# A two-stream decoder step: the sample's decode steps issued at another pace, the prompt's values multiplied over 512 columns

## The chip, the cores and the metric

One core of a Trainium2 chip runs one program. The metric is the device time of one execution in microseconds (us), read as the median of several runs of the same kernel.

## The reference

The program is one inference step of a two-layer decoder for two streams of tokens with the same weights (1024 channels, 16 heads of 64, 4096 hidden units). The **prompt** has 512 tokens, the **sample** 8 sequences of 4 new tokens, each with 2048 past keys and values in a paged cache. Layer 0 is a convolution module and an MLP. Then one key/value projection is made from the residual stream, and layer 1 is stick-breaking attention (query projection, attention, output projection) and another MLP. Cut to the part around the change:

```
k_flat, v_flat = split(x @ w_kv, 2)                 # x: after layer 0
q  = (x*(1+scale)+shift) @ attn_wq
z  = einsum('bqhd,bkhd->bhqk', q, k) * 64**-0.5 + bias[head]
log_rem = where(k_pos < q_pos, log_sigmoid(-z), 0)  # stick breaking, instead of a softmax
after   = exclusive suffix sum of log_rem over the keys
w  = where(k_pos < q_pos, exp(log_sigmoid(z) + after), 0)
o  = einsum('bhqk,bkhd->bqhd', w, v) @ attn_wo
x  = layer_norm(alpha*x + (1+gate)*o)               # post-norm; then the MLP in the same form
```

Everything is float32. The new keys and values of both streams are outputs too. scale, shift and gate come from small products of a condition vector with large matrices ("ada" below).

## The kernel before, in words

**Prompt.** Activations lie channel by channel: eight tiles of 128 channels by 512 tokens. To keep float32 accuracy each operand is split in two float32r parts, hi (a cast) and lo (the rest), and each product is three matmuls, hi*hi, hi*lo and lo*hi (`mm3`, L326 to L331; tile name `pd`). Weights come as 1 MB tiles `stage` (three buffers, loaded from ScalarE's DMA queue) and are split by `wsplit` (L312): ScalarE casts `whi` (L316), VectorE subtracts `wlo` (L319), two buffers each. `make_h` (L441) writes the split input of the next projection, `xhi` on ScalarE (L454), a helper `h` (L456), `xlo` on VectorE (L460); it takes the eight buffers of the projection before, so a block is written when its last reader is done.

The stages follow each other: convolution, LN (layer normalisation), `pw2`, LN, MLP 0 (eight blocks `fb`), LN, keys (K, eight tiles `pd`), values (V, L1346 to L1365), queries (Q), attention over eight head pairs (L1385 to L1441), output projection, LN, MLP 1 with a tail. The values are the one projection computed with tokens in the partitions: x is the stationary side and the weights are the moving side. They are made in four groups c of 256 columns; in each, for two pairs of token blocks, one PSUM bank `pv` takes two blocks of 128 tokens x 256 columns, with the eight blocks k of channels innermost. A bank is copied (`vN`, L1361) and written to two places in DRAM: `vd`, from which attention reads a head pair's values, and the output.

**Attention of a head pair** (a `pr`): TensorE makes the scores `pz` in three units of query blocks, ScalarE takes two sigmoids of them (L1414, L1416), VectorE a running product from the right (`TENSOR_TENSOR_SCAN`, L1423) and a product (L1424), TensorE transposes the weights (`awt`), ScalarE copies them (`aw`), TensorE multiplies with the values (`oP`), ScalarE and VectorE split the result (L1439, L1440).

**Sample.** Its dense layers stream large weights past 32 tokens. Its attention is a run of decode steps, four key steps and four value steps for each of the eight sequences. A key step `dec_keys` gathers two 1 MB tiles `kraw` from the cache (L1043, on GpSimd's queue; the same ring of four buffers that all the sample's weights use), transposes them on VectorE in eight pieces (`kt`, L1065) and makes scores `zt` with 64 matmuls (L1071). A value step `dec_values` gathers two tiles `vt` and makes 16 matmuls `av` (L1122). After four key steps `dec_weights` turns a sequence's scores into weights. Before the fourth sequence (counted from 0) 16 ada steps come (`ada_b_(1)`, `ada_a(1, 1)`: each a 1 MB load on SyncE's queue, and matmuls L246) whose results the prompt needs after attention. The transposes are ordered behind the last `xlo` of the last `make_h` (`latest_sub`), the decode matmuls behind the last prompt matmul noted in `latest`, which before is set by `mm3` alone, so not in the values or in attention.

**Order.** Both streams are Python generators, merged by two issue clocks (L1495 to L1509): each `yield` adds a cost to its stream's clock, and the stream whose clock is behind goes on. `DEC_COST` is the cost of a decode step, `SMP_COST` 2.9 that of a dense or ada step of the sample, `DN_COST` 5.2 that of a tile of a prompt projection, `AT_COST` that of a head pair, an MLP block costs 41.6. The costs so decide beside which prompt work a decode step is issued. Within that order a scheduler places each instruction when its planned inputs are ready; each engine then runs its own queue in order.

```
        i = 0 if (alive[0] and (not alive[1] or clock[0] <= clock[1])) else 1
        ...
            cost = next(gens[i])
        ...
                clock[i] += cost
```

Of the kernel before, what the change touches and what calls it, by code (L numbers as in the profile page):

```python
# [17 lines left out]
P = 128  # L18
D = 1024
KT = 8  # L20
# [7 lines left out]
CW = 31  # L28
NPG = 16
NPOOL = 160  # L30
DEC_COST = 10.0
CLK0 = -20.0
EARLY = 0
SMP_COST = 2.9
# [16 lines left out]
LN_COST = 16.0  # L51
DN_COST = 5.2
ML_COST = 2.6
AT_COST = 12.0
ALPHA = 4.0 ** 0.25
EPS = 1e-5
QSC = 0.125
# [54 lines left out]
def yoco_step_kernel(  # L112
# [9 lines left out]
    nc = tc.nc  # L122
    mm = nc.tensor.matmul
# [3 lines left out]
    dma = nc.sync.dma_start  # L127
# [14 lines left out]
    def pm(name="pm"):  # L142
        return ps.tile([P, 512], F32, tag="pm", bufs=3, name=name)

    def aux(name="aux"):
        return ps.tile([P, 512], F32, tag="aux", bufs=4, name=name)

    def lnp(name):
        return ps.tile([P, 512], F32, tag="ln", bufs=1, name=name)
# [7 lines left out]
    def tmp(name="tmp"):  # L157
        return pp.tile([P, 512], F32, tag="tmp", bufs=4, name=name)
# [145 lines left out]
    def wstage(src, k, queue=nc.scalar, after=None):  # L304
        st = wp.tile([P, 2048], F32, tag="stage", bufs=STB, name="stage")
        ins = queue.dma_start(st.rearrange("p (k c) -> p k c", k=k), src.rearrange("(k p) c -> p k c", p=P))
        if after:
            order(ins, after[-1])
            after.append(ins)
        return st.rearrange("p (k c) -> p k c", k=k)  # L310

    def wsplit(st, c0, cw, wp=wp, after=None, chain=None):  # L312
        k = st.shape[1]
        hi = wp.tile([P, k, cw], F32R, tag="whi", bufs=2, name="whi")
        lo = wp.tile([P, k, cw], F32R, tag="wlo", bufs=2, name="wlo")
        ins = nc.scalar.copy(hi, st[:, :, c0 : c0 + cw])  # L316
        if after:
            order(ins, after)
        ins = vec.tensor_tensor(lo, st[:, :, c0 : c0 + cw], hi.bitcast(F32), op=ALU.subtract)  # L319
        if chain is not None:  # L320
            in_turn(chain, ins)
        return hi, lo

    latest = []
# [8 lines left out]
    def order(ins, after):  # L333
        tc.add_manual_dep(ins.ins, after.ins.name,
                          mybir.DependencyInfo(mybir.DependencyClass.NoSync, mybir.DependencyReason.DATA), reason="issue order")
        return ins
# [76 lines left out]
    def in_turn(chain, ins):  # L413
        if chain:
            order(ins, chain[-1])
        chain.append(ins)
# [366 lines left out]
    for c in range(4):  # L783
        st = []
# [7 lines left out]
        accs = []  # L792
# [7 lines left out]
        if c == 0:  # L800
            p1c = ExitStack()
            plc = pool(p1c, "p1c", "right")
            accs = [pm("pw1") for _ in range(3)] + [aux("pw1")]
            ws = [None] * 4
# [36 lines left out]
            for k in range(KT):  # L841
                t = tmp("ax0")
# [11 lines left out]
        for i in range(2):  # L854
            kt = 2 * c + i
            if c:
                ws = [wsplit(st[o], i * P, P) for o in range(2)]
                accs = [pm("pw1") for _ in range(2)]
# [37 lines left out]
    for g in range(4):  # L896
        r = slice(32 * g, 32 * g + 32)
# [5 lines left out]
    def sample():  # L903
# [143 lines left out]
        def dec_keys(s, f, st):  # L1047
            if f == 0:
                qb = sq.tile([P, 2, 16, 8, NQ], F32, tag="qb", bufs=1, name="qb")
                for u in range(2):  # L1050
                    vec.tensor_tensor(
                        qb[:, u],
                        qr.rearrange("p (b t) -> p b t", t=32)[:, u * 16 : u * 16 + 16, s * 4 : s * 4 + 4].unsqueeze(2).to_broadcast([P, 16, 8, NQ]),
                        mqb.rearrange("p (b x q) -> p b x q", x=8, q=NQ), op=ALU.mult)
                st["qb"], st["zt"] = qb, [aux("zt") for _ in range(2)]
            qb, zt = st["qb"], st["zt"]
            raw = [ring("kraw") for _ in range(2)]
            for x in range(2):
                gather(raw[x], cache_k, krow[:, s, f, x : x + 1])
            for u in range(2):  # L1060
                for hh in range(2):
                    kt = sq.tile([P, 4, 256], F32, tag="kt", bufs=KTB, name="kt")
                    c0 = u * 512 + hh * 256
                    for x in range(2):
                        ins = vec.transpose(kt[:, 2 * x : 2 * x + 2, :], raw[x].rearrange("p (e c) -> p e c", e=2)[:, :, c0 : c0 + 256])  # L1065
                        if latest_sub and DBH:
                            order(ins, latest_sub[0])
                    for dd in range(2):
                        for g in range(4):
                            bl = g * 2 + dd  # L1070
                            behind(mm(  # L1071
                                zt[u][32 * g : 32 * g + 32, f * P : f * P + P],
                                qb[:, u, hh * 8 + bl].rearrange("p x q -> p (x q)"),
                                kt[:, :, bl * 32 : bl * 32 + 32],
                                start=(hh == 0 and dd == 0), stop=(hh == 1 and dd == 1), tile_position=(0, 32 * g)))
# [36 lines left out]
        def dec_values(s, a, st):  # L1112
            if a == 0:
                st["av"] = aux("av")
            av, wT = st["av"], st["wT"]
            for i in range(2):
                vt = ring("vt")
                gather(vt, cache_v, vrow[:, s, a, i : i + 1])
                for e in range(2):
                    for u in range(2):  # L1120
                        g = 2 * u + e
                        behind(mm(av[32 * g : 32 * g + 32, :], wT[u][:, i, e, a, :],  # L1122
                                  vt[:, e * D + u * 512 : e * D + u * 512 + 512],
                                  start=(a == 0 and i == 0), stop=(a == 3 and i == 1), tile_position=(0, 32 * g)))
            if a < 3:
                return
            am = sq.tile([P, 512], F32, tag="z_s", bufs=2, name="am")
            vec.tensor_tensor(am, av, bmask, op=ALU.mult)
            ot = aux("ot")
            for c in range(4):  # L1130
                mm(ot[:, c * 8 : c * 8 + 8], am[:, c * P : c * P + P], selq, start=True, stop=True)
            o = oT.rearrange("p (u c) t -> p u c t", u=2)[:, :, :, s * 4 : s * 4 + 4]
            vec.tensor_tensor(o, o, ot[:, 0:32].rearrange("p (c u q) -> p u c q", c=4, u=2), op=ALU.add)

        sts = [{} for _ in range(NS + 1)]
        for s in range(NS + 1):
# [5 lines left out]
            for f in range(4):  # L1142
                if s < NS:
                    dec_keys(s, f, sts[s])
                    yield DEC_COST
                if s > 0:
                    dec_values(s - 1, f, sts[s - 1])
                    yield DEC_COST
            if s < NS:
# [100 lines left out]
    def prompt():  # L1250
# [79 lines left out]
        nv_out = new_v_prompt[0].rearrange("(i p) h d -> p i (h d)", p=P)  # L1330
        vd_v = vd.rearrange("(i p) c -> p i c", p=P)
# [11 lines left out]
            dma(nk_out[:, ts.start // P : ts.stop // P, kt * P : kt * P + P], kn.rearrange("p (i c) -> p i c", i=n))  # L1343

        yield from p_dense_out(w_kv[:, 0:D], xhi, xlo, fink, first=H_0B)
        for c in range(4):  # L1346
            st = wstage(w_kv[:, D + c * 256 : D + c * 256 + 256], KT)
            ws = [wsplit(st[:, 4 * r : 4 * r + 4, :], 0, 256) for r in range(2)]
            for i2 in range(2):
                a = pm("pv")  # L1350
                for ii in range(2):
                    i = i2 * 2 + ii
                    o = a[:, ii * 256 : ii * 256 + 256]
                    for k in range(KT):
                        whi, wlo = [w[:, k % 4, :] for w in ws[k // 4]]
                        xh, xl = xhi[k][:, i * P : i * P + P], xlo[k][:, i * P : i * P + P]
                        mm(o, xh, whi, start=(k == 0), stop=False)
                        mm(o, xl, whi, start=False, stop=False)
                        mm(o, xh, wlo, start=False, stop=(k == KT - 1))
                t = tmp("vN")  # L1360
                nc.scalar.copy(t, a)  # L1361
                tv = t.rearrange("p (i c) -> p i c", i=2)
                dma(vd_v[:, 2 * i2 : 2 * i2 + 2, c * 256 : c * 256 + 256], tv)
                dma(nv_out[:, 2 * i2 : 2 * i2 + 2, c * 256 : c * 256 + 256], tv)
                yield DN_COST  # L1365
        yield from need("abA10")
        a10, b10 = mods["abA10"]
# [17 lines left out]
        for pr in range(KT):  # L1385
            qT, kT, vN = qts[pr], tmp("kTr"), tmp("vNr")
            dma(kT, kd[pr])
            vN = vN.rearrange("p (i c) -> p i c", i=4)
            dma(vN, vd_v[:, :, pr * P : pr * P + P])
            oP = lnp("oP")  # L1390
            for unit in units:
# [13 lines left out]
                for i, c0 in unit:  # L1405
                    for r, z in zip(halves, zs):
                        order(mm(z[:, c0 : c0 + (i + 1) * P], qT[r, i * P : i * P + P], kT[r, 0 : (i + 1) * P], start=False,
                                 stop=False, skip_group_check=True), head)
# [10 lines left out]
                for s, fx in sfs:  # L1419
# [8 lines left out]
                    w = att.tile([P, T], F32, tag="aw", bufs=2, name="aw")  # L1428
# [11 lines left out]
            vec.tensor_tensor(olo[pr], oP, ohi[pr].bitcast(F32), op=ALU.subtract)  # L1440
            yield AT_COST  # L1441
        p3.close()
# [55 lines left out]
    while any(alive):  # L1498
        i = 0 if (alive[0] and (not alive[1] or clock[0] <= clock[1])) else 1
# [42 lines left out]
```

## Time and profile before

| | |
|---|---|
| time, median of 3 runs | 1649.34 us (1648.95 to 1651.52) |
| the profiled execution | 1650.69 us; span from first to last instruction 1648.9 us |
| TensorE (PE) busy | 1553.3 us, 94% of the span |
| VectorE (DVE) busy | 954.8 us, 58% |
| ScalarE (ACT) busy | 569.4 us, 35% |
| mean granted TensorE clock | 0.979 of 2.4 GHz |
| DMA | 409.24 MB, mean 248 GB/s |

A busy time is the sum of an engine's instructions in a stretch, without counting overlaps twice. The granted clock is 1.0 at 2.4 GHz and 0.5 at 1.2 GHz; a value between is a mean over the stretch. In a row of a timeline, what stands in brackets is the time that the engine stood idle just before, and what ended it. Matmul ends are modelled, so the pace of matmuls is read from their starts.

### The profile page before, as it was taken

What the parts mean: (1) busy time and instruction counts of PE and PEld (TensorE: products, weight loads), DVE (VectorE), ACT (ScalarE), POOL (GpSimd) and SP (SyncE); (2) the same over time, 40 slices, a digit from 0 to 9 for tenths busy, and PEclk for the clock granted to TensorE, in tenths of its full rate; (3) what the DMA queues carried; (4) which work ended last, traced back from release to release, by engine and by line L of the source; (5) the groups of instructions that cost most, each with busy time, mean ns of one, the idle gap of its engine ahead of it and who ended that gap; (6) DMA issues with size and microseconds to landing.
All of it is one profiled execution on the core that took longest, in us unless ns stands there. A gap on an engine that the chain in (4) does not pass through costs nothing.

```text
span 1648.9 us, 25461 instructions
## 1 busy us (share of the span) xinstructions
PE 1553.3 (94%) x10489; PEld 1088.2 (66%) x10489; DVE 954.8 (58%) x1818; ACT 569.4 (35%) x907; POOL 181.2 (11%) x201
## 2 busy tenths in 40 slices
PE   6999989989999999999899999889889999999995
PEld 4666325656777777777478775557767767566885
DVE  4599545565676655655643448984765434233446
ACT  2322123261332233323332535852362323223342
POOL 1210200000012121110012113021111100000002
PEclk9999999999999999999999999999999999999998
DMA  9898879688667776676889878265546585885311
GB/s 327 279 329 305 230 283 368 246 325 309 225 232 266 272 270 239 224 253 226 343 282 331 281 272 313 96 241 193 193 154 239 185 335 182 352 339 180 96 62 51
DMA packets 152358, 409.24 MB, mean 248 GB/s; under 512 B 8197, under 2 KB 82213, under 8 KB 127651
## 3 DMA queue, kind: packets, MB, share of 16 engines
q1 hardware_dynamic: 50819, 161.86, 26.3%
q0 software_dynamic: 22944, 149.07, 25.2%
q10 hardware_dynamic: 78480, 96.70, 17.6%
q8 instruction: 82, 1.34, 0.3%
q14 instruction: 33, 0.27, 0.0%
HBM read 390.56 MB, written 17.88 MB: 248 GB/s over the span
## 4 chain that ended last, share of the span: by engine, by line
PE 78%; DMA 8%; issue 6%; DVE 5%; ACT 2%; POOL 1%; DVEq 0%; SPq 0%; POOLq 0%; ACTq 0%
PE pd L327 18%; PE pd L331 18%; PE pd L330 17%; PE zt L1071 3%; PE av L1122 3%; PE sd_acc L551 3%; PE cv L713 2%; DMA adaw<-in_ada_w_dram 2%; PE w_acc L578 1%; DMA kraw<-in_cache_k_dram,krow 1%; PE pw L327 1%; PE pw L330 1%; PE pw L331 1%; DMA stage<-in_conv_pw_w_dram 1%; PE ada_A L246 1%
## 5 line engine op out<-in xcount | busy, mean ns | idle before, releaser
L319 DVE TENSOR_TENSOR wlo<-stage,whi 128x1024 fp32r<-128x1024 f32 x184 | 223.1, 1215 | 216.8 <-ACT whi L316 216.4
L327 PE MATMUL pd<-xhi,whi 128*128 128x512 f32 (+1 forms) x832 | 321.4, 388 | 9.6 <-ACT whi L316 5.2
L316 ACT CAST whi<-stage 128x1024 fp32r<-128x1024 f32 x184 | 191.6, 1046 | 400.3 <-PE pd L331 350.6
L330 PE MATMUL pd<-xhi,wlo 128*128 128x512 f32 (+1 forms) x832 | 318.5, 384 | 2.7 <-DVE wlo L319 2.7
L331 PE MATMUL pd<-xlo,whi 128*128 128x512 f32 (+1 forms) x832 | 313.1, 386 | 5.6 <-DVE xlo L460 5.6
L1065 DVE STREAM_TRANSPOSE kt<-kraw 128x512 f32<-128x512 f32 x256 | 164.1, 685 | 138.8 <-DMA kraw<-in_cache_k_dram,krow 92.5
L327 PE MATMUL pd<-h2h,whi 128*128 128x512 f32 (+1 forms) x544 | 206.7, 388 | 1.6 <-DVE v L1240 1.0
L330 PE MATMUL pd<-h2h,wlo 128*128 128x512 f32 (+1 forms) x544 | 205.0, 382 | 0.0
L331 PE MATMUL pd<-h2l,whi 128*128 128x512 f32 (+1 forms) x544 | 205.0, 383 | 0.0
L327 PEld LDWEIGHTS pd<-xhi,whi 128*128 128x128 f32 x832 | 160.7, 193 | 59.7 <-issue 13.7
L331 PEld LDWEIGHTS pd<-xlo,whi 128*128 128x128 f32 x832 | 156.5, 192 | 61.1 <-issue 18.2
L330 PEld LDWEIGHTS pd<-xhi,wlo 128*128 128x128 f32 x832 | 160.9, 193 | 42.1 <-issue 10.8
L1240 DVE SCALAR_TENSOR_TENSOR v<-pd,mod_B,v 128x512 f32<-128x512 f32 x120 | 87.8, 745 | 114.1 <-PE pd L331 113.9
L1043 POOL DMA_INDIRECT kraw<-in_cache_k_dram,krow x64 | 66.3, 1035 | 621.1 <-DVE kt L1065 387.9
L327 PEld LDWEIGHTS pd<-h2h,whi 128*128 128x128 f32 x544 | 101.9, 188 | 34.8 <-issue 10.4
L1215 ACT ACTIVATE relu<-pd 128x512 f32<-128x512 f32 (+1 forms) x68 | 38.9, 572 | 239.7 <-PE pd L331 222.3
L331 PEld LDWEIGHTS pd<-h2l,whi 128*128 128x128 f32 x544 | 101.8, 188 | 28.8 <-issue 9.4
L330 PEld LDWEIGHTS pd<-h2h,wlo 128*128 128x128 f32 x544 | 102.2, 188 | 25.0 <-issue 6.7
L1043 POOL DMA_INDIRECT vt<-in_cache_v_dram,vrow x64 | 70.3, 1098 | 273.4 <-PE av L1122 222.9
L1071 PE MATMUL zt<-kt,qb 128*32 128x128 f32 x2048 | 76.8, 279 | 8.2 <-DVE kt L1065 7.7
L1071 PEld LDWEIGHTS zt<-kt,qb 128*32 128x32 f32 x2048 | 52.8, 110 | 33.2 <-issue 16.4
L368 DVE BATCH_NORM_STATS2 bn<-lnT 128x6 f32<-128x128 f32 x160 | 36.5, 284 | 60.0 <-PE lnT L366 59.8
(300 smaller groups left out, 1987.7 us busy)
## 6 DMA issues: line engine op xcount, KB each, us to landing
sw<-in_mlp_w_dram SPq DMA_DIRECT2D x64, 1024.0 KB
stage<-in_mlp_w_dram ACTq DMA_DIRECT2D x64, 1024.0 KB
adaw<-in_ada_w_dram SPq DMA_DIRECT2D x40, 1024.0 KB
stage<-in_conv_pw_w_dram ACTq DMA_DIRECT2D x10, 1024.0 KB
adaw<-in_ada_w_dram SPq DMA_DIRECT2D x16, 512.0 KB
swkv<-in_w_kv_dram SPq DMA_DIRECT2D x8, 1024.0 KB
stage<-in_w_kv_dram ACTq DMA_DIRECT2D x8, 1024.0 KB
ur<-ud POOLq DMA_DIRECT2D x24, 270.0 KB, 8.0
```

Source lines behind the costliest of these rows:

```text
L316: ins = nc.scalar.copy(hi, st[:, :, c0 : c0 + cw])
L319: ins = vec.tensor_tensor(lo, st[:, :, c0 : c0 + cw], hi.bitcast(F32), op=ALU.subtract)
L327: first = mm(out, whi, xh, start=start, stop=False)
L330: mm(out, wlo, xh, start=False, stop=False)
L331: latest[:] = [mm(out, whi, xl, start=False, stop=stop)]
L551: mm(acc[32 * g : 32 * g + 32, :], hT[:, kk * 2 + kp, :], blk[:, kp * D + c * 512 : kp * D + c * 512 + 512], start=(kk == 0), stop=(kk == ...
L1043: nc.gpsimd.indirect_dma_start(out=out, out_offset=None, in_=cache.rearrange("g (r e) h d -> (g r) (e h d)", e=2), in_offset=bass.Indirect ...
L1065: ins = vec.transpose(kt[:, 2 * x : 2 * x + 2, :], raw[x].rearrange("p (e c) -> p e c", e=2)[:, :, c0 : c0 + 256])
L1071: behind(mm(zt[u][32 * g : 32 * g + 32, f * P : f * P + P], qb[:, u, hh * 8 + bl].rearrange("p x q -> p (x q)"), kt[:, :, bl * 32 : bl * 3 ...
L1122: behind(mm(av[32 * g : 32 * g + 32, :], wT[u][:, i, e, a, :], vt[:, e * D + u * 512 : e * D + u * 512 + 512], start=(a == 0 and i == 0), ...
L1215: latest_act[:] = [act(r, a, AF.Relu)]
L1240: ins = vec.scalar_tensor_tensor(v[kt][:, ts], a, gt[:, kt, 8:9], v[kt][:, ts], op0=ALU.mult, op1=ALU.add)
```

## The change

Three edits. A decode step costs 9.2 units on the sample's issue clock, not 10.0, and a head pair of attention 4.0 on the prompt's, not 12.0. The values are made in two groups of 512 columns: four banks (three `pm` and the `ln` bank) take one block of 128 tokens each, the channel blocks k go outermost in pairs, each pair with its own split of 2 x 512 weight columns, and all four token blocks use it before the next pair. There is one yield per pair, eight in all, as before. The last matmul of each product goes into `latest`. Each bank is copied and written out once, as 128 rows of 512 columns.

```diff
-DEC_COST = 10.0
+DEC_COST = 9.2
...
-AT_COST = 12.0
+AT_COST = 4.0
...
-        for c in range(4):
-            st = wstage(w_kv[:, D + c * 256 : D + c * 256 + 256], KT)
-            ws = [wsplit(st[:, 4 * r : 4 * r + 4, :], 0, 256) for r in range(2)]
-            for i2 in range(2):
-                a = pm("pv")
-                for ii in range(2):
-                    i = i2 * 2 + ii
-                    o = a[:, ii * 256 : ii * 256 + 256]
-                    for k in range(KT):
-                        whi, wlo = [w[:, k % 4, :] for w in ws[k // 4]]
+        for c in range(2):
+            cols = slice(c * 512, c * 512 + 512)
+            accs = [pm("pv") for _ in range(3)] + [lnp("pv")]
+            for k0 in range(0, KT, 2):
+                if k0 % 4 == 0:
+                    st = wstage(w_kv[k0 * P : k0 * P + 512, D + c * 512 : D + c * 512 + 512], 4)
+                whi, wlo = wsplit(st[:, k0 % 4 : k0 % 4 + 2, :], 0, 512)
+                for i, a in enumerate(accs):
+                    for kk in range(2):
+                        k = k0 + kk
                         xh, xl = xhi[k][:, i * P : i * P + P], xlo[k][:, i * P : i * P + P]
-                        mm(o, xh, whi, start=(k == 0), stop=False)
-                        mm(o, xl, whi, start=False, stop=False)
-                        mm(o, xh, wlo, start=False, stop=(k == KT - 1))
-                t = tmp("vN")
-                nc.scalar.copy(t, a)
-                tv = t.rearrange("p (i c) -> p i c", i=2)
-                dma(vd_v[:, 2 * i2 : 2 * i2 + 2, c * 256 : c * 256 + 256], tv)
-                dma(nv_out[:, 2 * i2 : 2 * i2 + 2, c * 256 : c * 256 + 256], tv)
+                        mm(a, xh, whi[:, kk, :], start=(k == 0), stop=False)
+                        mm(a, xl, whi[:, kk, :], start=False, stop=False)
+                        latest[:] = [mm(a, xh, wlo[:, kk, :], start=False, stop=(k == KT - 1))]
+                    if k0 == KT - 2:
+                        t = tmp("vN")
+                        nc.scalar.copy(t, a)
+                        dma(vd_v[:, i, cols], t)
+                        dma(nv_out[:, i, cols], t)
                 yield DN_COST
```

## Rows read from the trace of the kernel before

**Rows 1.** The page: busy time by engine; one group of instructions with its mean ns.

```profile
PE 1553.3 (94%) x10489; PEld 1088.2 (66%) x10489; DVE 954.8 (58%) x1818; ACT 569.4 (35%) x907; POOL 181.2 (11%) x201
...
L319 DVE TENSOR_TENSOR wlo<-stage,whi 128x1024 fp32r<-128x1024 f32 x184 | 223.1, 1215 | 216.8 <-ACT whi L316 216.4
...
L316 ACT CAST whi<-stage 128x1024 fp32r<-128x1024 f32 x184 | 191.6, 1046 | 400.3 <-PE pd L331 350.6
```

**Rows 2.** Busy time by stretch: length, PE, PEld, DVE, ACT, POOL, granted clock, DMA share, GB/s.

```profile
560.00:760.00 200.00, 200.00 (x1372) 152.15 (x1371) 116.21 (x167) 61.48 (x85) 29.20 (x28) 1.00 0.68 241
...
796.00:812.00 16.00, 11.77 (x86) 4.97 (x84) 11.65 (x48) 3.17 (x7) 0.00 (x0) 0.99 1.03 416
812.00:836.00 24.00, 23.18 (x110) 13.22 (x111) 19.38 (x32) 15.91 (x22) 4.51 (x4) 0.86 0.86 310
...
875.00:934.00 59.00, 58.68 (x592) 52.20 (x580) 22.28 (x29) 14.31 (x19) 11.14 (x10) 1.00 0.92 330
934.00:945.00 11.00, 7.35 (x16) 4.83 (x17) 7.26 (x9) 11.00 (x17) 0.00 (x0) 0.69 0.50 149
...
1034.00:1076.00 42.00, 33.29 (x349) 22.22 (x348) 40.49 (x72) 32.31 (x65) 0.00 (x0) 0.98 0.21 66
```

**Rows 3.** Timeline of PE: start, duration, in keys (512 columns), then values (256).

```profile
862.06 0.39 PE L331 MATMUL pd<-xlo,whi 128*128 128x512 f32 x1
...
865.01 0.39 PE L327 MATMUL pd<-xhi,whi 128*128 128x512 f32 x1
...
880.85 0.28 PE L1357 MATMUL pv<-whi,xhi 128*128 128x256 f32 x1
...
888.65 0.28 PE L1359 MATMUL pv<-wlo,xhi 128*128 128x256 f32 x1
```

**Rows 4.** The same, from the last value matmul into the queries.

```profile
933.40 0.28 PE L1359 MATMUL pv<-wlo,xhi 128*128 128x256 f32 x1
934.42 0.50 PE L327 MATMUL pd<-xhi,whi 128*128 128x512 f32 x1 [0.74 <-ACT whi L316]
...
944.54 0.53 PE L327 MATMUL pd<-xhi,whi 128*128 128x512 f32 x1
```

**Rows 5.** Timeline of ACT there.

```profile
934.28 2.92 ACT L454 ACTIVATE xhi<-v,b_A,a_A 128x512 fp32r<-128x512 f32 x4
...
938.52 1.51 ACT L456 ACTIVATE h<-v,b_A,a_A 128x512 f32<-128x512 f32 x2
```

**Rows 6.** Timeline of PE: attention's first scores.

```profile
996.07 0.29 PE L1397 MATMUL pz<-maskx,maskw 64*128 64x128 bf16 x4
```

**Rows 7.** Timeline of DVE: the last instruction of a head pair, four of the eight.

```profile
1019.51 0.68 DVE L1440 TENSOR_TENSOR xlo<-oP,xhi 128x512 fp32r<-128x512 f32 x1
...
1036.77 0.67 DVE L1440 TENSOR_TENSOR xlo<-oP,xhi 128x512 fp32r<-128x512 f32 x1
...
1071.19 0.66 DVE L1440 TENSOR_TENSOR xlo<-oP,xhi 128x512 fp32r<-128x512 f32 x1
...
1128.46 0.69 DVE L1440 TENSOR_TENSOR xlo<-oP,xhi 128x512 fp32r<-128x512 f32 x1 [7.17 <-ACT xhi L1439]
```

**Rows 8.** Attention: L1065 alone (length, DVE busy), and DVE's longest wait (total, times, longest).

```profile
996.00:1130.00 134.00, 28.42 (x44) 0.97 0.55 205
...
DVE kt L1065 <- DMA kraw<-in_cache_k_dram,krow: 14.0, 5, 4.6
```

**Rows 9.** Timeline of PE among the keys: a value step, half a key step.

```profile
865.77 1.92 PE L1122 MATMUL av<-vt,wT 128*32 128x512 f32 x16
...
874.19 1.08 PE L1071 MATMUL zt<-kt,qb 128*32 128x128 f32 x32
```

**Rows 10.** The same before the keys: ada steps of eight records, the first two key tiles.

```profile
796.21 1.06 PE L246 MATMUL ada_B<-adaw,cT 128*32 128x512 f32 x8
...
812.82 0.79 PE L327 MATMUL pd<-xhi,whi 128*128 128x512 f32 x1 [1.63 <-ACT xhi L454]
...
831.08 0.39 PE L331 MATMUL pd<-xlo,whi 128*128 128x512 f32 x1
```

## The prediction

> **What bounds the kernel now.** I read the page first: TensorE is busy 94% of the span [rows 1]. Then the table of stages [rows 2]: a column that says 200.00 of 200.00 us for PE means that every microsecond of matmul put there is a microsecond of time, and one that says 7.35 of 11.00 is a hole, where work is free and the wait is what counts. The stages around the change are of both kinds. The first MLP (560 to 760) and the values (58.68 of 59) are full. The hole at 934 to 945, between values and queries, has PE busy 7.35 at a granted clock of 0.69, that is 6.8 of 11 us at 1.2 GHz instead of 2.4. The hole before the keys (796 to 812) has 11.77 of 16. Attention, 1034 to 1076, has 33.29 of 42, with DVE at 40.49: there DVE is the bound, not PE. So a part counts by whether it takes matmul time from a full stage, or closes a hole, or moves work from the one kind to the other.
>
> **1. Values over 512 columns.** Now 384 matmuls of 256 columns; one starts every (888.65 - 880.85) / 65 = 0.120 us [rows 3]. Then 192 of 512, which in the keys start every (865.01 - 862.06) / 13 = 0.227 us. 384 x 0.120 = 46.1, 192 x 0.227 = 43.6: **-2.5 us**, in a full stage. The Trainium skill ("TensorE: Matmul & The Clock Gate", section "Back-to-back issue gap") gives 262 cycles for 256 columns and 518 for 512, so a fixed part of 6 cycles; by that the estimate would be 192 x 6 / 2.4 GHz = 0.5 us saved, and the rows' fixed part, 13 ns, is five times as large, so the rows decide.
> Cost against it: eight casts (1.05 us) and subtractions (1.22 us) as before [rows 1], each now for 24 matmuls of 512 (5.4 us) with a second buffer pair free since the step before. I take them as hidden; if one pair is never free early, the stage pays 8 x 2.3 = 18 us. All three pm banks and the ln bank are held; their readers (row statistics before the keys, queries after) are over or take the first bank 18 matmuls after its sum is complete, so I take 0. The bytes are the same, in rows twice as long; steps of the sample issued within the eight values yields are four, as now.
>
> **2. The hole between values and queries.** Now all eight row blocks of x are read up to the last i, so make_h can write a new xhi only at the very end. The last value matmul starts at 933.40; the next one waits 0.74 us for a cast, and up to 944.54 there are 14 of them [rows 4]: 14 x 0.227 = 3.2 us of work in 944.54 - 933.52 = 11.0 us, **7.8 us lost**, half clock included. With k outermost, blocks 0 to 5 are read for the last time 24 matmuls (5.4 us) or more before the end, 0 and 1 three steps before (16 us). ScalarE needs 0.8 us a block for xhi and as much for h [rows 5], and has room for six blocks (9.6 us) in those 16 us. After the last value matmul there remain two blocks (3.2 us), one copy of a sum (0.6) and a cast (1.05): 4.9 us, plus 0.7 for the last subtraction, against 5.2 us until the queries' first tile asks for block 7. I take 6.5 us of the 7.8 back. Ends: all 7.8, or 0 if the four sums, copied together into the four tmp buffers that h also takes, hold h until their writes land.
>
> **3. Fewer sample steps in attention.** I walked both issue clocks. Eight attention yields are worth 96 units now, and 32 then. Between the first and the last of them ten decode steps are issued now (keys 5.2, 5.3, 6.0, 6.1, 6.2 and five value steps), then three (values 4.3, keys 6.0, values 5.0). Four of the others (keys 5.2 and 5.3, values 4.1 and 4.2) come before attention and three (keys 6.1 and 6.2, values 5.1) after it.
> What attention gives back: it runs from 996.07 to 1129.15 [rows 6, 7], 133 us. Three head pairs that no key step touches end 34.42 us apart, 1036.77 to 1071.19: 11.5 each. The first, with 9 us of transposes in its 23.4, would need about 14. Undisturbed: 14 + 7 x 11.5 = 94, so the sample costs 39 us there. Transposes for key steps take 28.42 us of DVE in it [rows 8], 44 of them; the scans and products of dec_weights, of qb and of am some 7 more; and DVE stands 14.0 us in five waits for a gather that is not there yet, with attention's own scans queued behind it. Then: 8 transposes of keys 6.0 and 0 to 8 of keys 5.3, with the same 7 us: 12 to 18 us of DVE instead of 35, and fewer late gathers, since a gather now has most of attention to land. 18 to 26 us come back; I take 23.
> What it costs: the steps go to full stages. A key step is two gathers on POOL, 8 transposes and 64 matmuls, 2 x 1.0 us, a value step two gathers and 16 matmuls, 1.85 [rows 9]; 0.2 to 0.3 us more for each change of stream. 4 x 2.3 + 3 x 2.1 = 15.5 us. The DVE part is hidden there (116 of 200 busy in 560 to 760), and the POOL queue waits for buffers, not the reverse. Net **-7.5 us**, between -2.5 and -10.5.
>
> **4. The closer pace takes filler out of the hole before the keys.** With 9.2 in place of 10, the third sequence is done earlier, so the 16 ada steps before the fourth (one 1 MB load on SP's queue, eight matmul records of 1.07 us in all) begin during the last MLP block instead of at its end. Now twelve of them run from 796.21 to right behind the second key tile, which ends at 831.3 [rows 10]; then three are issued there, and nine, 9.6 us, in the full MLP. The first key matmul, at 812.82, waits for xhi, not for ada, so the hole itself gives little back (0 to 3). The first two key tiles, 812.82 to 831.3 with four ada steps among them, would be limited by their own 48 matmuls (10.9 us and the half rate's 3.4) or by ScalarE at 8 x 1.6 = 12.8 us: 4 back. 9.6 - 4 - 1.6, the middle of 0 to 3, is net **+4 us**, between +2 and +7. The granted clock of 812 to 836 is 0.86, so 6.7 us of it at 1.2 GHz, right behind the hole [rows 2]. The Trainium skill (the same page, section "HAM oscillation") says that matmuls which come back after an idle stretch run at half rate; the row agrees, and by that rule less filler would mean more time at 1.2 GHz, by an estimate one or two us of loss more.
> At the LN after the output projection, dec_weights of sequence 6 and keys 7.0 lie among the LN's DVE work now, keys 6.3 and the same weights then: 0, plus or minus 3.
>
> **Sum.** -2.5 - 6.5 - 7.5 + 4 = -12.5 us on the profiled execution's 1650.69 us (span 1648.9): 1638.2. The median of the runs is 1.35 us below that execution, so 1637.
>
> **Rivals.** (a) Attention gives back only what the others pay, because its three nearly full engines (33.3, 40.5 and 32.3 of 42 us) trade places. Then -2.5 - 6.5 + 4 = -5: 1644. For it: PE is at 79% there even without key steps. Against: the step from 11.5 us a pair to 19.1 (1071.19 to 1128.46, three pairs) where keys are issued. (b) The late gathers vanish altogether and the LN hole costs nothing: -2.5 - 7.8 - 13 - 1 = -24: 1625. For it: 14.0 us of waits, and 7.2 at the last xlo. (c) Slower: the holes do not shrink when their filler leaves. 25 us of matmuls (9.6 + 15.5) go to full stages; if the LN hole returns nothing and attention half of 23, this is 25 - 11.5 - 9 = +4.5: 1654. It decides from the point where both holes return less than 16 of the 25 us. For it: attention's last pair waits 7.2 us for ScalarE, a chain that fewer steps need not shorten. (d) The values stage stalls on its casts because ScalarE, in order, has make_h or copies of sums before them: 1 to 2 us in each of eight steps, so 8 to 16 on my sum: 1645 to 1653.
>
> **How the numbers follow.** My forecast has a chance of 0.54, with its own range 1630 to 1643; (a) 0.18, (b) 0.10, (c) 0.10, (d) 0.08. 0.2% is 3.3 us, about what a measurement of this kernel can tell from no change: 1646.0 to 1652.6 counts as no change. The forecast and (b) are faster, and two thirds of (a) with a little of (d): 0.78. The same: a third of (a), half of (d) and a little of (c): 0.13. Slower: 0.09. The range from 1626 to 1649 leaves out (c), half of (b) and a part of (d), 2 in 10.
>
> **What would show it.** Right: value matmuls of 512 columns 0.227 us apart; no stretch near 0.69 clock between values and queries, and queries starting within 1.5 us of the last value; attention, from its first pz to its last xlo, in 105 to 116 us; the stages that took its steps and the ada steps some 25 us longer in sum. Wrong: attention above 122 us; idle PE inside the values; the stretch from the last MLP matmul to the first key matmul over 24 us. The forecast itself fails with a time above 1646.

## The result: slower, by 0.5%

The changed kernel took 1660.21 us (median of four, 1655.35 to 1660.75) beside 1649.14 us for the kernel before: a ratio of 1.0054, 95% interval 1.0030 to 1.0079. Measured again beside later experiments it was 1658.25 us, 1.0049 (1.0023 to 1.0075). The forecast was 1637, the range ended at 1649. Its profiled execution is the shortest of its four, 1655.35 us, so the table below explains 4.7 us; the other three spent more time at a low clock (mean 0.972, not 0.975).

Stages are cut at the starts of matmuls (an MLP from its first to its last matmul with `h2h` or `h2l`; attention: first `pz` to last `xlo`); a decode step is counted where its matmuls ran, half a key step as 0.5.

| stage | before | after | decode steps | ada steps |
|---|---|---|---|---|
| start to MLP 0 | 372.4 us | 368.9 | | |
| MLP 0 | 423.5 | 435.5 | 28, 28 | 4, 12 |
| hole before the keys | 16.9 | 18.8 | 0, 0 | 6, 4 |
| keys | 62.4 | 66.9 | 2.5, 6 | 6, 0 |
| values | 58.2 | 52.2 | 4.5, 2.5 | |
| gap to the queries | 1.0 | 0.2 | | |
| queries | 61.6 | 67.6 | 4, 5.5 | |
| attention | 133.1 | 117.6 | 10, 4 | |
| to MLP 1 | 97.2 | 96.6 | 6, 6 | |
| MLP 1 | 405.0 | 411.7 | 9, 12 | |
| rest | 17.5 | 17.5 | | |

The first row is not the change's work: the same matmuls run there in every kernel, and it took 369 to 377 us in the profiles of all runs, with 20 to 41 us of it at half clock. The stages behind it lose 8.1 us.

At 2.2 us a step [rows 9], moved steps explain the changes from attention's end on, all but 2.3 us of attention's 15.5, and 4.4 of the values' 6.0. Two places lose: MLP 0 with the hole and the keys, +18.4 us, of which 3.5 decode steps are 7.7, so **10.7 us too much**; and the queries, +6.0 with 3.3 us of steps, **2.7 too much**, while the gap in front of them gave 0.8 back; 6.5 were to be gained there.

The first place. Stretches of the changed kernel (length, PE, PEld, DVE, ACT, POOL, granted clock, DMA share, GB/s): the hole, the first two key tiles, values, the queries' start, and the stretch behind it.

```profile
804.50:823.30 18.80, 11.42 (x71) 6.52 (x69) 12.85 (x51) 4.03 (x8) 3.99 (x4) 0.78 0.80 307
823.30:841.00 17.70, 15.68 (x80) 11.83 (x80) 16.82 (x31) 12.51 (x18) 0.00 (x0) 0.75 0.02 6
890.00:942.00 52.00, 52.00 (x328) 40.84 (x325) 26.33 (x40) 19.60 (x27) 5.67 (x7) 1.00 0.76 273
942.00:952.00 10.00, 10.00 (x81) 7.01 (x80) 6.34 (x10) 9.03 (x13) 3.64 (x4) 1.00 0.97 353
952.00:968.00 16.00, 6.34 (x58) 4.58 (x56) 6.17 (x10) 7.28 (x10) 1.90 (x2) 0.80 1.05 399
```

PE in the hole of the changed kernel, answering [rows 10]: the two spreads of the LN's statistics, the first key matmuls.

```profile
815.13 2.07 PE L386 MATMUL mb<-dg,onesm 128*128 128x128 f32 x8 [2.08 <-DVE dg L385]
819.56 2.08 PE L386 MATMUL rb<-dg,onesm 128*128 128x128 f32 x8 [2.36 <-DVE dg L385]
823.26 0.79 PE L327 MATMUL pd<-xhi,whi 128*128 128x512 f32 x1 [1.63 <-ACT xhi L454]
...
826.98 1.22 PE L331 MATMUL pd<-xlo,whi 128*128 128x512 f32 x2 [1.65 <-DVE xlo L460]
```

Every one of these waits ends on VectorE or ScalarE: the LN's own chain. VectorE has three instructions for each block (L420, L421 and `xlo`). From the first product with `rb` to the last `xlo` they take 14.7 us, before and after alike (before, then after):

```profile
811.23 0.69 DVE L421 TENSOR_TENSOR v<-v,rb 128x512 f32<-128x512 f32 x1 [1.05 <-PE rb L386]
...
823.48 2.49 DVE L460 TENSOR_TENSOR xlo<-h,xhi 128x512 fp32r<-128x512 f32 x4
```

```profile
821.67 0.69 DVE L421 TENSOR_TENSOR v<-v,rb 128x512 f32<-128x512 f32 x1 [1.97 <-PE rb L386]
...
833.93 2.49 DVE L460 TENSOR_TENSOR xlo<-h,xhi 128x512 fp32r<-128x512 f32 x4
```

From the last MLP matmul to the start of the third key tile it takes 36.5 us, with half a key step at its end; before, with eight ada steps more in it, 37.8. Eight steps left and 1.3 us came back: the way to the first `xlo` matmul got 1.7 us longer (22.5 us, not 20.8; the two spreads ran at 1.2 GHz and took 2.07 us each, not 1.16), and from there to the end of the second tile it got 2.1 us shorter (12.6, not 14.8); the rest lies behind the second tile.

The second place. ScalarE and its DMA queue (ACTq) at the queries' start; PE's next matmul.

```profile
945.11 0.38 ACTq L306 DMA_DIRECT2D stage<-in_attn_wq_dram  x1
...
952.52 0.38 ACTq L486 DMA_DIRECT2D axd<-v  x1
...
953.23 0.48 ACTq L486 DMA_DIRECT2D axd<-v  x1
...
957.62 8.44 ACTq L486 DMA_DIRECT2D axd<-v  x5
966.16 1.04 ACT L316 CAST whi<-stage 128x1024 fp32r<-128x1024 f32 x1 [8.72 <-DMA axd<-v]
```

```profile
967.25 0.80 PE L327 MATMUL pd<-xhi,whi 128*128 128x512 f32 x1 [9.66 <-ACT whi L316]
```

`make_ax` (L486) writes eight blocks of 256 KB to DRAM from ScalarE's queue (the spill), behind the last 1 MB weight load of the queries, issued at 945.11. The row of five spans 8.44 us, but each issue takes 0.3 to 0.4 us; most of the row is a wait of 6.3 us between the first of the five and the second:

```profile
957.62 0.34 ACTq L486 DMA_DIRECT2D axd<-v  x1
...
964.28 1.78 ACTq L486 DMA_DIRECT2D axd<-v  x4
```

A transfer raises a semaphore, a counter, when it has landed, and a few semaphores serve all transfers in turn. By the trace's semaphore records that second write uses the one of the weight load next, and waits until the load has landed, at 964.21, 19.1 us after its issue. In order behind it stood the cast of the queries' next weights, and PE stood 9.66 us and then ran 10.2 us at 1.2 GHz. In the kernel before the load was issued at 939.43 and landed at 945.58, 6.1 us later and before that write was due, and the eight issues took 0.3 to 0.6 us each. Why the load took three times as long isn't shown; the DMA engines were nearly full behind it in both (a share of 0.95 or more).

Attention: first `pz`, and the ends of pairs 1, 2, 5, 6 and 8, answering [rows 6, 7].

```profile
1010.13 0.23 PE L1397 MATMUL pz<-maskx,maskw 64*128 64x128 bf16 x1
```

```profile
1035.15 0.68 DVE L1440 TENSOR_TENSOR xlo<-oP,xhi 128x512 fp32r<-128x512 f32 x1
...
1046.77 0.68 DVE L1440 TENSOR_TENSOR xlo<-oP,xhi 128x512 fp32r<-128x512 f32 x1
...
1078.68 0.67 DVE L1440 TENSOR_TENSOR xlo<-oP,xhi 128x512 fp32r<-128x512 f32 x1
...
1097.06 0.67 DVE L1440 TENSOR_TENSOR xlo<-oP,xhi 128x512 fp32r<-128x512 f32 x1
...
1126.98 0.69 DVE L1440 TENSOR_TENSOR xlo<-oP,xhi 128x512 fp32r<-128x512 f32 x1 [9.09 <-ACT xhi L1439]
```

Pairs 2 to 5 take 10.9 us each; the first still takes 25, the sixth (with the key step) 18.4, and the eighth, from 1108.51 on, 18.5 with 9.09 of wait, longer than the 7.17 of before.

### The profile page after: what moved, and what is told of

Its sections match the earlier page's. It is cut to its first block, busy times and chain, and to the rows that moved or that the text cites. A ratio compares the mean times of both kernels' runs of the same rounds, so it can differ in the third digit from the quotient of the medians.

```text
span 1653.6 us, 25074 instructions
## 1 busy us (share of the span) xinstructions
PE 1553.2 (94%) x10297; PEld 1078.5 (65%) x10297; DVE 956.5 (58%) x1818; ACT 568.5 (34%) x907; POOL 179.7 (11%) x201
## 4 chain that ended last, share of the span: by engine, by line
PE 79%; DMA 8%; issue 7%; DVE 4%; ACT 1%; POOL 0%; DVEq 0%; SPq 0%; POOLq 0%; ACTq 0%
PE pd L327 18%; PE pd L330 17%; PE pd L331 17%; PE zt L1071 3%; PE av L1122 3%; PE sd_acc L551 3%; PE cv L713 2%; DMA adaw<-in_ada_w_dram 2%; DMA kraw<-in_cache_k_dram,krow 2%; PE w_acc L578 1%; PE pw L327 1%; PE pw L330 1%; PE pw L331 1%; DMA stage<-in_conv_pw_w_dram 1%; PE ada_A L246 1%
## 5 line engine op out<-in xcount | busy, mean ns | idle before, releaser
L1065 DVE STREAM_TRANSPOSE kt<-kraw 128x512 f32<-128x512 f32 x256 | 163.6, 685 | 136.6 <-DMA kraw<-in_cache_k_dram,krow 88.7
L331 PEld LDWEIGHTS pd<-xlo,whi 128*128 128x128 f32 x832 | 157.7, 194 | 55.6 <-issue 13.8
L1071 PEld LDWEIGHTS zt<-kt,qb 128*32 128x32 f32 x2048 | 52.4, 110 | 29.6 <-issue 15.8
```

What stands on the lines that cost most here:

```text
L331: latest[:] = [mm(out, whi, xl, start=False, stop=stop)]
L1071: behind(mm(zt[u][32 * g : 32 * g + 32, f * P : f * P + P], qb[:, u, hh * 8 + bl].rearrange("p x q -> p (x q)"), kt[:, :, bl * 32 : bl * 3 ...
```

## The experiments

Each has its median and its ratio to the kernel before, run on the same chip.

**Which of the three edits** (e1 to e4): the changed kernel with one or two of them taken back.

```diff
 e1 values alone            DEC_COST = 10.0  AT_COST = 12.0
 e2 costs alone             DEC_COST = 9.2   AT_COST = 4.0   old values
 e3 values and decode cost  DEC_COST = 9.2   AT_COST = 12.0
 e4 values and pair cost    DEC_COST = 10.0  AT_COST = 4.0
```

> The values over 512 columns alone, both costs as before. Theory 1 (the costs lose the time: filler leaves the hole before the keys, and attention returns only what it exports): the values stage 52 us instead of 58, the idle stretch behind it closed, a total of 1640 to 1645 us. Theory 2 (the values edit brings the wait of ScalarE behind its own DMA queue between values and queries, which costs what the edit saves): 1646 to 1650 us, with the queries' stage again some 6 us longer than the 61.6 of before. Theory 3 (the values edit is the whole loss): 1657 us or more.

> Both costs of the change, the values as before. Theory 1: +8 to +12 us on before, 1657 to 1661. If the two parts are independent and the values edit gains 5, then 1665. Theory 3 (the values edit is the loss): 1647 to 1651. Attention about 117 us, the hole before the keys at a clock of 0.8 for 17 us, under theory 1.

> The values over 512 columns and the decode cost 9.2, a head pair's cost 12.0 as before. Theory 1: the hole before the keys loses as in the changed kernel (the first MLP about 435 us, 19 us to the first key matmul at a low clock); attention is at 125 to 135 us but its steps no longer stand elsewhere: 1652 to 1658. Rival (the loss is that attention's steps were moved to full stages): 1643 to 1648.

> The values over 512 columns and a head pair's cost 4.0, a decode step at 10.0 as before. Theory 1 (attention returns only what it exports, and the filler in the hole before the keys stays as before): 1643 to 1649, attention 114 to 120 us, the first MLP 423 us. Rival (the attention cost is the loss): 1654 to 1660.

| | median us | ratio | interval |
|---|---|---|---|
| e1 | 1648.6 | 0.9992 | 0.9968 to 1.0016 |
| e2 | 1664.27 | 1.0074 | 1.0045 to 1.0103 |
| e3 | 1661.72 | 1.0070 | 1.0047 to 1.0092 |
| e4 | 1649.73 | 0.9987 | 0.9971 to 1.0002 |

The loss comes with 9.2 from the start (e2, e3) and is absent without it (e1, e4). The values are not the loss (theory 3 falls), but alone they gain nothing that can be measured: e1 is in the range of its theory 2, but not for that theory's reason, as its queries take 60.4 us and ScalarE's queue has no such wait. e1's trace shows another. ScalarE, then PE, at the end of its values:

```profile
938.79 5.38 ACT L456 ACTIVATE h<-v,b_A,a_A 128x512 f32<-128x512 f32 x7 [3.89 <-DMA out_dram<-vN]
```

```profile
934.99 0.49 PE L330 MATMUL pd<-xhi,wlo 128*128 128x512 f32 x1 [1.42 <-DVE wlo L319]
...
940.38 0.72 PE L331 MATMUL pd<-xlo,whi 128*128 128x512 f32 x1 [3.13 <-DVE xlo L460]
```

The four sums lie in the buffers that `h` needs until their writes land, so a part of the old hole stays; values to queries take 115.7 us instead of 120.9 (with half a key step less). Attention takes 138.6 us there instead of 133.1 (with half a key step more), which takes it all back.

**ScalarE's queue** (f1 to f3): the spill goes to SyncE's queue, in the changed kernel, in e1 and in the kernel before.

```diff
-                nc.scalar.dma_start(spill[k], t)
+                dma(spill[k], t)
```

> The changed kernel with one edit: the eight spill writes behind the values (axd) go to SyncE's queue instead of ScalarE's. In the changed kernel ScalarE stood 8.7 us in issuing five of them, TensorE waited 9.7 us for the next cast, and the granted clock fell to half for 10.2 us. Theory 1 (that wait is on the path): 9 to 15 us less than the changed kernel, 1645 to 1651. Rival (the cast would have waited for the stage load or VectorE anyway): within 3 us of 1660.

> The values over 512 columns alone, with the spill writes on SyncE's queue, both costs as before. Theory 1: if the values edit alone brings ScalarE's wait, this gains on it 9 to 15 us and is at 1635 to 1639, faster than either kernel; if the wait belongs to the costs, it equals the values edit alone, 1640 to 1645.

> The kernel before with the spill writes on SyncE's queue: they were issued in 0.33 to 0.55 us each there, so no change is expected, 1647 to 1651. Less than 1645 would mean that ScalarE's queue held the path in the kernel before as well.

f1: 1653.09 us, 1.0011 (0.9992 to 1.0031); the queries take 58.8 us instead of 67.6 and no time at half clock. The stretch, and the casts right behind the eight blocks:

```profile
957.00:973.00 16.00, 14.44 (x122) 10.17 (x125) 7.98 (x12) 7.66 (x11) 1.95 (x2) 1.00 1.05 403
```

```profile
957.03 5.74 ACT L484 ACTIVATE v<-v,aln 128x512 f32<-128x512 f32 x8
...
962.68 1.98 ACT L316 CAST whi<-stage 128x1024 fp32r<-128x1024 f32 x2
```

The DMA engines are as full as before, and the weight load takes 19.0 us to land; but now SyncE's queue waits for it, and the casts don't stand behind it. That wait was on the path: by the ratios f1 takes back 6 to 7 us of a loss of 8 to 9, though not the 9 to 15 that theory 1 asked for. f2 (1651.49 us, 1.0000, 0.9980 to 1.0021) and f3 (1651.93, 1.0004, 0.9989 to 1.0019) gain nothing: without 9.2 it isn't there. It is not the only loss, for e2, with 9.2 and the old values, has no such wait (its load landed after 5.1 us) and loses 0.7%.

**The filler** (f4, g1, g2): f4 keeps 10.0 up to the ada steps and 9.2 behind them; g1 delays the ada steps alone in the changed kernel; g2 hastens them in the kernel before.

```diff
 f4
         for s in range(NS + 1):
+            DEC_COST = 10.0 if s < ADA_AT else 9.2
 g1 (g2 in the kernel before, with -24.0 and 24.0)
             if s == ADA_AT:
+                yield 25.6
...
                     yield from ada_a(1, 1)
+                yield -25.6
```

> The changed kernel with the decode cost at 10.0 up to the ada steps and 9.2 after them, so that the ada steps lie in and behind the hole before the keys as before. Theory 1 (the loss is in that hole and in the first MLP): the first MLP back at about 424 us, the hole with its keys about 3 us longer than now but 9 us less in all than the two in the changed kernel: 1650 to 1654. Rival (the hole returns what leaves it, the loss is elsewhere): within 3 us of 1660.

> The changed kernel; only the sixteen ada steps are issued 25.6 units of the sample's clock later, and the clock is set back behind them, so that decode steps stay on their closer pace. The filler is back in the hole before the keys and in the first key tiles. Theory 1 (the hole gives nothing back for filler that leaves it): 8 to 12 us less than the changed kernel, 1648 to 1652, the first MLP 8 to 9 us shorter, the hole and the two first key tiles no longer than 36 us, less half clock there than 17 us. Rival (the order of the decode steps is what costs): 1657 to 1663.

> The kernel before; only the sixteen ada steps are issued 24 units of the sample's clock earlier, in the last block of the first MLP, and the clock is set back behind them; the decode steps stay where they were. Theory 1: the loss of the change appears without the change: 8 to 12 us above before, 1659 to 1663, the hole and the first two key tiles still 35 us, with 14 to 17 us of half clock. Rival (the hole shrinks when its filler leaves, as the prediction had it for 5.6 of 9.6 us): 1651 to 1656.

f4: **1639.58 us, 0.9931 (0.9909 to 0.9953)**, faster than both kernels, and 10 us better than my theory had it. MLP 0 takes 423.6, the hole 17.3 with 0.3 us at half clock, the queries 57.9 without the wait (the last load of their weights goes out at 933.48 and lands 13.6 us later; PE then waits 0.64 us for the cast), attention 110.9. g1: 1651.99, 1.0009 (0.9992 to 1.0025), a time as theory 1 said. MLP 0 is 9 us shorter; hole and keys take 85.6 us in both, with eight ada steps more in g1 but two decode steps fewer. The hole and two tiles are at 40.0 us and not at the 36 forecast, so not all of the filler is free there. ScalarE's wait went with it: PE waits 0.86 us for the same cast, not 9.66.

```profile
964.23 0.50 PE L327 MATMUL pd<-xhi,whi 128*128 128x512 f32 x1 [0.86 <-ACT whi L316]
```

g2: 1655.28, 1.0015 (0.9998 to 1.0033), tells nothing, because the steps did not move. PE's first ada steps in the kernel before, in g2 and in the changed kernel:

```profile
786.16 1.06 PE L246 MATMUL ada_B<-adaw,cT 128*32 128x512 f32 x6
```

```profile
786.43 1.06 PE L246 MATMUL ada_B<-adaw,cT 128*32 128x512 f32 x6
```

```profile
759.62 3.64 PE L246 MATMUL ada_B<-adaw,cT 128*32 128x512 f32 x32
```

They start some 23 us behind the start of the last value step (763.00, 763.27, 736.1), whatever the issue clock says. It isn't their loads: the first goes out at 752.29 and 752.56 in the first two, 34 us before the matmuls. What holds the matmuls there was not tried.

**The clock or the chain** (j1, with the changed kernel again as a1): 21 matmuls whose results nobody uses keep PE at work in the hole.

```diff
+        def idle_work(self, after, n):
+            d = aux("idle")
+            for j in range(n):
+                order(mm(d[:, 0:P], onesm, ident, start=True, stop=True), after)
```

> The changed kernel, with 21 added matmuls of 128 columns (0.29 us each at full clock, results unused) in the hole before the keys: three before the last transposes of the LN, six before and seven behind the spread of the means, five behind the spread of the deviations. They do nothing but keep TensorE at work. Theory 1 (the hole loses because its filler is gone and the clock falls at 815.0 for 17.1 us): half clock there 0 to 7 us instead of 17, the spreads at 1.16 us instead of 2.08, the stretch from the last MLP matmul to the first value matmul 80 to 83 us instead of 85.7, 3 to 6 us less in all than the changed kernel, 1654 to 1657. Rival (the LN's chain on VectorE alone sets the hole, whatever TensorE does): 84 to 88 us for that stretch, 1658 to 1663.

> The changed kernel again, beside the three others on one chip, as the yardstick for their small differences: 1658 to 1662, with the hole before the keys again at half clock for 14 to 17 us.

Hole and first two key tiles in a1, then in j1 (columns as above), and PE in j1:

```profile
808.50:826.40 17.90, 10.53 (x71) 5.71 (x69) 12.83 (x51) 4.02 (x8) 3.99 (x4) 0.84 0.84 323
826.40:844.00 17.60, 15.58 (x81) 11.56 (x81) 16.84 (x31) 12.54 (x18) 0.00 (x0) 0.77 0.02 7
```

```profile
811.20:828.10 16.90, 14.03 (x112) 9.63 (x110) 12.05 (x47) 3.96 (x8) 3.99 (x4) 1.00 0.88 337
828.10:846.50 18.40, 15.25 (x80) 11.73 (x80) 17.24 (x35) 12.54 (x18) 0.00 (x0) 0.81 0.04 10
```

```profile
821.84 1.16 PE L394 MATMUL mb<-dg,onesm 128*128 128x128 f32 x8 [0.74 <-DVE dg L393]
822.83 1.73 PE L379 MATMUL idle<-c,onesm 128*128 128x128 f32 x14
825.35 1.16 PE L394 MATMUL rb<-dg,onesm 128*128 128x128 f32 x8 [0.80 <-DVE dg L393]
...
832.11 1.22 PE L331 MATMUL pd<-xlo,whi 128*128 128x512 f32 x2 [2.77 <-DVE xlo L474]
```

j1: 1658.12 us, 1.0046 (1.0029 to 1.0063); a1: 1658.25: nothing is gained that can be measured. The clock stays at 1.00 through the hole and the spreads take 1.16 us, so the first `xlo` matmul starts 20.9 us behind the last MLP matmul, where it was 21.6 in a1 (one spread at half clock) and 22.5 in the changed kernel's first profile (both). But the clock falls in the key tiles instead (0.81), and from there they take 13.0 us, not 12.5; of 13.8 us at half clock 7.0 stay, so j1 tests the hole alone. For the tiles other runs tell: from the first `xlo` matmul to the end of the second tile, f1, a1, e3 and e2 take 12.5 to 12.6 us, with 3.1, 4.4, 4.6 and 4.7 us of that at half clock. There VectorE's chain sets the length. My theory had the clock as a main part of the price; it is at most some 2 us, in the hole.

**The rest** (h1, i2 to i4): e1 without noting value matmuls in `latest`; f4 with `AT_COST = 12.0`; f4 with the old values; g1 with the spill on SyncE's queue.

> The values over 512 columns alone, both costs as before, and the last matmul of each value product not noted in latest, so that decode matmuls are not ordered behind the values, as in the kernel before. The values edit alone gained 4 us in the values and 1 in the queries, but its attention took 138.5 us instead of 132 to 133. If the noted matmuls push decode steps into attention: attention back at 131 to 134 us and 1641 to 1645 in all. If attention is longer for another reason (the transfers of the values): 137 to 139 us and 1647 to 1650.

> The kernel with the closer pace only behind the ada steps (1639.6 us), with a head pair's cost 12.0 again instead of 4.0. With ten decode steps in attention instead of four. If attention returns only what it exports: 1637 to 1643. If fewer steps in attention were a gain of their own, once the hole before the keys is in order: 1646 to 1652, attention 130 us or more and the stages behind it 10 to 13 us shorter.

> The closer pace behind the ada steps and a head pair's cost of 4.0, but the values over 256 columns as in the kernel before; with the values over 512 columns it was 1639.6 us. If the values edit is worth what it saves in its own stage and in the queries' half clock: 1644 to 1649. If, as alone (1648.6 against 1650.9), it is worth 2 us or less: 1639 to 1643.

> The changed kernel with both repairs: the ada steps issued 25.6 units later (1652.0 us alone) and the spill writes on SyncE's queue (1653.1 us alone). Theory 1 (two separate losses): both gains add up, 1644 to 1648. Rival (one loss behind both, such as the time at which the loads come): no better than either alone, 1650 to 1654.

| | median us | ratio | interval |
|---|---|---|---|
| h1 | 1654.17 | 1.0008 | 0.9988 to 1.0028 |
| i2 | 1651.43 | 1.0002 | 0.9982 to 1.0022 |
| i3 | 1644.28 | 0.9967 | 0.9954 to 0.9981 |
| i4 | 1652.41 | 1.0007 | 0.9989 to 1.0025 |

h1's attention is 139.8 us: noting the matmuls isn't what lengthens it. i3 against f4: the values are worth some 5 us once nothing stalls behind them. i2 against f4: the pair's cost is worth some 12 us there, though between e1 and e4 it is worth nothing. i4 gains nothing on g1, as its rival had it, and the trace of g1 tells why: there ScalarE's wait was gone already. The queries are 2.7 us shorter, attention is 3.0 longer with 20.5 us at half clock instead of 13.7.

Why e4 and f4 differ in attention (120.5 and 110.9 us) is seen in a head pair without any decode step: pairs 3 to 7 have none in either and take 62.1 and 52.4 us. Stretches of one pair in e4 and f4, then ScalarE in each:

```profile
1049.80:1062.20 12.40, 9.52 (x96) 6.19 (x92) 9.96 (x18) 9.54 (x20) 0.00 (x0) 1.00 0.15 44
```

```profile
1043.80:1054.20 10.40, 9.37 (x93) 5.97 (x93) 9.95 (x18) 9.26 (x20) 0.00 (x0) 1.00 0.17 49
```

```profile
1050.38 1.26 ACT L1414 ACTIVATE afx<-pz,bias_p 128x512 f32<-128x512 f32 x2
1051.53 0.48 ACT L1429 COPY aw<-awt 128x384 f32<-128x384 f32 x1
1051.89 0.71 ACT L1416 ACTIVATE as<-pz,bias_p 128x512 f32<-128x512 f32 x1
1053.51 0.48 ACT L1429 COPY aw<-awt 128x384 f32<-128x384 f32 x1 [0.91 <-PE awt L1427]
1053.89 0.69 ACT L1416 ACTIVATE as<-pz,bias_p 128x512 f32<-128x512 f32 x1
```

```profile
1043.24 0.71 ACT L1415 ACTIVATE afx<-pz,bias_p 128x512 f32<-128x512 f32 x1
1043.82 0.71 ACT L1417 ACTIVATE as<-pz,bias_p 128x512 f32<-128x512 f32 x1
1044.39 0.72 ACT L1415 ACTIVATE afx<-pz,bias_p 128x512 f32<-128x512 f32 x1
1044.96 0.73 ACT L1417 ACTIVATE as<-pz,bias_p 128x512 f32<-128x512 f32 x1
1045.53 0.91 ACT L1430 COPY aw<-awt 128x384 f32<-128x384 f32 x2
```

The busy times are nearly the same; the scheduler put the same instructions in another order. In e4 a second sigmoid `as` is queued behind a copy that waits for PE, in f4 all four sigmoids come first. The two differ by 2 us a pair, 9.7 over the five, about as much as the attentions do. That the order makes the difference is read from the traces; no run changed it alone, and what makes the scheduler choose one or the other was not tried.

## Why the prediction was wrong

**Values (step 1): right.** Value matmuls of the changed kernel on PE, 29 starts apart, (901.40 - 894.82) / 29 = 0.227 us; PE is busy 52.00 of 52 us; no stall on casts, so rival (d) is out. In e1, with the same steps, the stage is 3.3 us shorter for the 2.5 forecast.

```profile
894.82 0.40 PE L1357 MATMUL pv<-whi,xhi 128*128 128x512 f32 x1
...
901.40 0.39 PE L1359 MATMUL pv<-wlo,xhi 128*128 128x512 f32 x1
```

**The hole to the queries (step 2): failed.** The old hole closed as described (queries 0.2 us behind the last value matmul), but the step counted what it removed and not what is queued next on ScalarE: the spill's eight writes, one of which waits until the last weight load has landed. That is 9.66 us of idle PE, and gap and queries lost 1.9 us where 6.5 were to be won. In e1 the low end that the step named, `h` held by the sums' writes, was what happened (3.89 us).

**Attention (step 3): mis-sized.** 23 us were to come back and 15.5 did, for six steps that ran elsewhere (13.2 us; my walk of the clocks had seven): net -2.3, not -7.5. I counted VectorE's transposes as time; the last pair's wait for ScalarE stayed, and the first pair kept its two steps.

**The hole before the keys (step 4): failed.** Nine ada steps were to leave and 5.6 of their 9.6 us to come back. Eight left, MLP 0 grew by 12.1 us (1.5 a step with the changes of stream, where the step took 1.07), and 1.3 came back. "The first two key tiles would be limited by their own 48 matmuls" or by ScalarE at 12.8: they took 16.4 us (823.26 to 839.61), bound by VectorE's chain through `xlo`, which the step left out: 16.82 of 17.70 busy. The fall of the granted clock was forecast rightly: 17.1 us at 1.2 GHz against 6.8 before. The Trainium skill ("TensorE: Matmul & The Clock Gate", section "HAM oscillation") has matmuls at half rate after an idle stretch; the trace agrees, 815.13 at 2.07 us against 1.16 in j1. What it cost was small, at most some 2 us by j1 and a1.

On the profiled execution step 2 missed by 8.4 us (1.9 lost for 6.5 won), step 4 by 6.7 (10.7 for 4) and step 3 by 5.2; against a sum of -12.5 no one of them turns the sign alone.

So it went in part as rival (c), given 0.10: the hole before the keys does not shrink when filler leaves. Against its bar of 16 of 25 us both holes returned about 17 of 22, just over it, but the wait on ScalarE's queue, which no rival had, came on top. None of the signs of wrong came (18.8 < 24, 117.6 < 122, no idle PE in the values). Of the signs of right, 0.227 and 0.2 us came; attention missed its 116, and the stages that were to grow by some 25 us in sum grew by 29.3: MLP 0 12.1, keys 4.5, queries 6.0, MLP 1 6.7.

Open: why the weight load took 19.1 us, and why attention takes 5.5 us longer in e1 and 3.0 in i4. In both, attention has more half clock than its partner, which may be cause or effect.

## What to carry to other kernels

Filler that runs in a hole set by another engine is nearly free as long as it fits, and moving it into a full stage costs its whole length; ask of a hole which engine's chain gives its length before counting anything back. A DMA issued from a compute engine's queue is an instruction of that engine, and can wait there for an earlier transfer: look what load is ahead of it and what cast is behind it. A pace that is right for one part of a stream can be wrong for another: 9.2 from the ada steps on gave 1639.6 us, the same number from the start 1660.2.

## What the runs showed of the hardware that was not expected

A 256 KB write, 0.3 us to issue, stood 6.3 us in ScalarE's queue until a 1 MB load with the same semaphore had landed, 19.1 us after that load's issue; with the writes on SyncE's queue and the DMA engines as busy (1.05 against 1.05), ScalarE's casts went on. And a head pair with nearly the same busy times on every engine took 10.4 or 12.4 us, with a few instructions on ScalarE in another order.
